# Two-layer hybrid mixer kernel: the gate matmuls of the recurrent part from fp32 to three fp32r passes, and their place in the order

## The chip, the cores and the metric

The kernel runs on one core of a Trainium2 chip, as one program. The metric is the device time of one execution in microseconds. The engines are TensorE (PE in the profile; PEld are its weight loads), VectorE (DVE), ScalarE (ACT), GpSimd (POOL) and SyncE (SP), which issues most of the DMAs.

## The reference

A backbone of two layers over 1024 latent tokens and 256 context tokens, width 1024. Each layer normalizes and modulates its input, projects it to 2048 columns, mixes tokens in three parallel ways, projects back, and runs a gated feed-forward part with a convolution. Context tokens run through the first layer fully; in the second only their keys, values and recurrent states are needed. The change is in the recurrent mixer, 512 channels wide:

```python
u = dwconv(r, conv_w, conv_b, 2, 1)                  # r: first 512 projected columns
for d, reverse in enumerate((False, True)):          # two directions
    r_ = sigmoid(blockdiag(u, w_a[d]) + b_a[d])      # 8 blocks of 64 x 64
    i_ = sigmoid(blockdiag(u, w_x[d]) + b_x[d])
    log_a = -8 * r_ * softplus(-lam[d]);  a = exp(log_a)
    h[d] = scan(a, sqrt(1 - exp(2 * log_a)) * i_ * u)   # h_t = a_t h_(t-1) + drive_t
y = (h[0] + h[1]) * gelu(gate)                       # gate: next 512 projected columns
```

The two other mixers are attention: one global, one over a window, with two key/value heads and four query heads each.

## The kernel before

Tokens lie along the free axis: 256 of context (chunk c), then two chunks of 512 latent tokens (A and B), 1280 in all (TOK). Most matmuls compute fp32 products in three passes: each operand is split into a high part, rounded to fp32r by a ScalarE copy, and a low part, the rest, by a subtraction on VectorE or GpSimd (`split`, L319); `gemm` (L326) adds high x high, high x low and low x high into one PSUM bank.

`in_proj` (L853) holds the stage in question. It goes over four channel tiles `ct` of 128 channels. Each has two projections of 24 matmuls per chunk: the raw half (i even) and the gate half (i odd). `lru_evac` copies the raw half from PSUM into `lru_raw`, and the gate half through a Gelu into `lru_gate`. `lru_conv` makes `u` from the raw half (one ScalarE activation and three VectorE operations for each of two token ranges). `lru` runs both directions: for each, two gate products of `u` with the block-diagonal weights `bd` in three chunks (L817, fp32 matmuls, banks 4 and 5 in turn), each evacuated by a tanh, then activations and VectorE operations, ending in the scan. `lru_out` adds the directions (L841) and multiplies by the gate (L842). In layer 1 both leave the context columns out.

Then four groups of head columns are projected, token by token tile (ten tiles of 128 tokens; groups 0 and 2 leave out the two context tiles in layer 1): group 0 gives the queries `gq`, group 1 keys and values `gk` and `gv`, groups 2 and 3 go to DRAM by way of `st`. Each tile is 24 matmuls of 256 columns and one or two evacuations. Attention follows; its first score products (out of `K` and `Q`) are the end of the stage.

Banks 0 to 3 take the projections: in the order 3, 0, 1, 2 for the channel tiles (L886), 0, 1, 2, 3 for the head groups. In the first tile chunk A of projections 0, 1 and 2 is done first, in banks 0, 1 and 2; the third of these (the raw half of the second tile) is evacuated late, by the `late` entry.

On-chip memory is laid out by hand. In the region X0, slots of 5120 bytes hold: slot 0 the raw half, slot 1 `u`, slot 2 the gate, slots 3 to 6 in turn the three work tiles A, B and C of a direction. There is one raw, one `u` and one gate slot, so each waits for its last reader of the tile before. Behind slot 6, at X0 + 35872, lies `mraw`, the buffer for modulation weights (`mod_fill`, 24 steps of PE work that are put among the others as fillers; their results are used in the output projection). In the region H0, eight slots of 5120 bytes hold the residual `h`. It is saved to DRAM (`save`) so that its slots can be reused: `bd` in slots 6 and 7, the recurrent result `ya` in 0 to 3, `gq` in 4 and 5, `gk` in 6, `gv` in 7. Group 1's weights for the second half of the rows lie at X0 and X0 + 35872 (`ex`, L868).

The order on each engine is not that of the text. A scheduler takes the instructions with the text's order as priority, and its own estimate of when each is ready, and writes one fixed sequence per engine and DMA queue; it inserts the waits that overlapping memory needs. On the chip each engine goes through its sequence in order.

Of the kernel before, what the change touches and what calls it, by code (L numbers as in the profile page):

```python
# [9 lines left out]
F32 = mybir.dt.float32  # L10
F32R = mybir.dt.float32r
# [5 lines left out]
P = 128  # L17
# [4 lines left out]
TOK = SEQ + CTX  # L22
# [269 lines left out]
class Builder:  # L292
# [378 lines left out]

    def mod_fill(self):
        for s in (*range(16, 32), *range(40, 48)):
            self.mod_step(0, s, self.sb("mraw", [P, 1024], F32, self.X0 + 35872) if s < 32 else None)
            yield

    def rstd_from(self, out, v, t):
# [72 lines left out]

    def load_bd(self, l):
        nc = self.nc
        bd = self.sb("bd", [P, 2, 2, 4, P], F32, self.H0 + 6 * 5120)
        nc.gpsimd.memset(bd, 0.0)
        for a, name in ((0, "lru_w_a"), (1, "lru_w_x")):
            for o in range(2):
                for d in range(2):
                    src = self.io[name][l, d].rearrange("(t o) c e -> o c t e", o=2)[o]
                    nc.sync.dma_start(bd[64 * o:64 * o + 64, a, d, :, 64 * o:64 * o + 64], src)
        self.bd = bd  # L760

    def proj(self, l, i, ch, x, w, ring):
        n = CHUNKS[ch][1]
# [38 lines left out]
                self.stt(u[:, c0:c0 + n], r[:, p0 + s:p0 + s + n], cw(i), u[:, c0:c0 + n], OP.mult, OP.add)  # L802
        return u

    def lru(self, l, ct, u):
        nc = self.nc
        lc = self.lcol[:, l]
        hs = []
        for d in range(2):
            j = 4 * d + ct  # L810
            A, B, C = (self.lslot(3 + (self.lru_i + q) % 4) for q in range(3))
            self.lru_i += 3
            for dst, a in ((A, 0), (B, 1)):
                for ch in ("c", "A", "B"):
                    c0, n = CHUNKS[ch]
                    ps = self.bank((4, 5))
                    self.mm(ps[:, :n], self.bd[:, a, d, ct], u[:, c0:c0 + n], True, True)  # L817
                    self.act(dst[:, c0:c0 + n], ps[:, :n], AF.Tanh, scale=0.5, bias=lc[:, a, j:j + 1])
            self.act(C, A, AF.Tanh, scale=lc[:, 2, j:j + 1], bias=lc[:, 2, j:j + 1])
            self.act(A, A, AF.Exp, scale=lc[:, 3, j:j + 1], bias=lc[:, 3, j:j + 1])  # L820
            self.stt(C, A, 1.0, C, OP.add, OP.mult)
            nc.vector.tensor_scalar(A, C, -1.0, 1.0, op0=OP.mult, op1=OP.add)
            self.stt(C, A, 1.0, C, OP.add, OP.mult)
            self.act(C, C, AF.Sqrt, scale=0.25)
            self.stt(B, B, 1.0, u, OP.add, OP.mult)
            nc.vector.tensor_tensor(B, B, C, op=OP.mult)
            scan = nc.vector.tensor_tensor_scan
            if d == 0:
                scan(C, A, B, 0.0, OP.mult, OP.add)
            else:  # L830
                scan(C[:, :CTX][:, ::-1], A[:, :CTX][:, ::-1], B[:, :CTX][:, ::-1], 0.0, OP.mult, OP.add)
                scan(C[:, CTX:][:, ::-1], A[:, CTX:][:, ::-1], B[:, CTX:][:, ::-1], C[:, 0:1], OP.mult, OP.add)
            hs.append(C)
        self.hs = hs
# [18 lines left out]
    def in_proj(self, l, x, wc, fillers):  # L853
# [4 lines left out]
        def save(ks):  # L858
            c0 = 0 if need else CTX
            for k in ks:  # L860
                nc.sync.dma_start(self.hsp[k][:, c0:], self.h[k][:, c0:])

        save((6, 7))
        self.load_bd(l)
        wp = {}

        def load(grp):
            ex = {1: (self.X0, self.X0 + 35872), 3: (self.X0 + 10240, self.X0 + 14336)}  # L868
            wp[grp] = [self.weight(win[:, 4 * q:4 * q + 4, 1024 + 256 * grp:1280 + 256 * grp], 4, 256,
                                   ex[grp] if q and grp in ex else (None, None), pool_lo=grp != 1)  # L870
                       for q in range(2)]

        done = set()
        for ct in range(4):
            for i in (2 * ct, 2 * ct + 1):
                if i not in wc:
                    wc[i] = self.lru_weight(l, i)
                if i == 7:
                    load(0)
                for ch in ("A", "B", "c"):  # L880
                    if ch == "c" and i % 2 and not need:
                        continue
                    for i2 in ((0, 1, 2) if (i, ch) == (0, "A") else (i,)):
                        if (i2, ch) not in done:
                            done.add((i2, ch))
                            ps = self.proj(l, i2, ch, x, wc[i2], (i2,) if (i, ch) == (0, "A") else (3, 0, 1, 2))  # L886
                            if (ct, i2) == (0, 2):
                                late = ps
                            else:
                                self.lru_evac(l, *ps)  # L890
                    if ch != "B":
                        next(fillers, None)
                if i % 2 == 0:
                    u = self.lru_conv(l, ct)
                    if ct == 0:
                        self.lru_evac(l, *late)
                    self.lru(l, ct, u)
                    save(((0,), (1, 4), (2, 5), (3,))[ct])
            self.lru_out(l, ct)
            if l == 0 and ct == 1:  # L900
                for _ in self.params_load(1, self.MS0):
                    pass
                self.lru_cols(1)
# [3 lines left out]
        for grp in range(4):  # L907
# [4 lines left out]
            for tt in range(10):  # L912
# [3 lines left out]
                o = (tt if tt < 2 else (tt - 2) % 4) * P  # L916
                ps = self.bank((0, 1, 2, 3))[:, :256]
                i = 0
# [612 lines left out]
```

## Time and profile before

| what | value |
|---|---|
| median of 3 runs | 3006.15 us (3005.23 to 3008.45) |
| the profiled execution: its time | 3004.2 us |
| its span, first to last instruction | 3002.4 us |
| mean granted TensorE clock | 0.981 of full speed |
| busy: PE, DVE, ACT, POOL | 94%, 72%, 50%, 45% |
| recurrent part with head groups, layer 0 | about 92 to 363 us |
| the same, layer 1 | about 1698 to 1948 us |

The busy share is an average over stages with different limits. Idle time that a view shows stands ahead of an instruction, with the engine whose signal ended it. A line number may be that of a helper: L308 is every activation, L311 every matmul, L317 every scalar_tensor_tensor of VectorE, so instructions are told apart by the names of what they write and read: `bank<-lru,bd` is a gate matmul, `bank<-w,a` a head group's matmul on latent tokens, `bank<-w,ac` on context tokens, `bank<-a,w` and `bank<-ac,w` a channel tile's projection, `lru` any tile of the recurrent part. A fp32 matmul shows as two instructions. Where a row merges several instructions (x2), its shape is that of the first.

### The profile page before, as it was taken

How to read it: one execution, taken by the hardware profiler on the slowest of the kernel's cores; microseconds unless marked ns; L12 is line 12 of the kernel's file. 1: busy time of each engine (PE TensorE's matmuls, PEld its weight loads, DVE VectorE, ACT ScalarE, POOL GpSimd, SP SyncE). 2: the span in 40 equal slices, each digit the busy share in tenths (PEclk: the TensorE clock that was granted, in tenths of full speed). 3: DMA queues.
4: the chain of work that ended last, by engine and by line, in shares of the span. 5: the costliest groups of instructions: out<-in, count | busy, mean ns of one | idle time of the engine just before them, and what ended most of it. 6: DMA issues, size and time to landing. Idle time of an engine off the chain costs nothing. (4 is left out here: it accounts for less than half of the span.)

```text
span 3002.4 us, 38806 instructions
## 1 busy us (share of the span) xinstructions
PE 2823.1 (94%) x14523; PEld 2265.2 (75%) x14523; DVE 2156.1 (72%) x2890; ACT 1497.1 (50%) x2426; POOL 1354.4 (45%) x814
## 2 busy tenths in 40 slices
PE   7999988899899999999999989988998999999998
PEld 4668955668788888887778768956676788887887
DVE  5666798775876666676756766898727877776666
ACT  4675477843433333365542666378834433344114
POOL 1211166642455555547773210067652666666110
PEclk8999999999999999999999999999999999999999
DMA  7422200132333333375452211200031344335321
GB/s 267 142 65 92 78 1 18 37 105 75 106 111 111 111 111 111 111 246 169 160 185 85 73 33 36 74 22 11 22 123 60 114 125 124 119 122 196 106 77 57
DMA packets 295774, 299.56 MB, mean 100 GB/s; under 512 B 16586, under 2 KB 250658, under 8 KB 295586
## 3 DMA queue, kind: packets, MB, share of 16 engines
q1 hardware_dynamic: 271538, 246.59, 26.0%
q10 hardware_dynamic: 24048, 50.50, 4.8%
q8 instruction: 114, 1.87, 0.3%
q14 instruction: 74, 0.61, 0.1%
HBM read 243.02 MB, written 54.02 MB: 99 GB/s over the span
## 5 line engine op out<-in xcount | busy, mean ns | idle before, releaser
L322 POOL TENSOR_TENSOR w<-wr,w 128x1024 fp32r<-128x1024 f32 (+1 forms) x220 | 565.5, 2593 | 220.1 <-ACT w L308 198.2
L311 PE MATMUL bank<-y,w 128*128 128x512 f32 (+1 forms) x2688 | 576.0, 374 | 14.6 <-DVE h L317 12.7
L311 PEld LDWEIGHTS bank<-y,w 128*128 128x128 f32 x2688 | 468.4, 191 | 111.6 <-DVE h L317 15.4
L311 PE MATMUL bank<-xt,w 128*128 128x512 f32 x2112 | 513.2, 396 | 23.2 <-ACT p L308 8.0
L311 PEld LDWEIGHTS bank<-xt,w 128*128 128x128 f32 x2112 | 398.8, 191 | 115.4 <-POOL w L322 9.7
L1131 POOL TENSOR_TENSOR ph<-pf,ph 128x512 fp32r<-128x512 f32 x256 | 340.3, 1351 | 299.2 <-PE bank L311 178.0
L317 DVE SCALAR_TENSOR_TENSOR h<-bank,mod,h 128x512 f32<-128x512 f32 (+1 forms) x448 | 300.1, 685 | 188.8 <-PE bank L311 188.0
L317 DVE SCALAR_TENSOR_TENSOR cv<-fr,fcol,cv 128x1282 f32<-128x1282 f32 (+1 forms) x176 | 375.4, 2190 | 70.0 <-ACT cv L308 70.0
L308 ACT ACTIVATE w<-wr 128x1024 fp32r<-128x1024 f32 (+1 forms) x220 | 222.8, 1016 | 393.1 <-POOL wr L178 234.6
L311 PE MATMUL bank<-a,w 128*128 128x512 f32 x1536 | 387.8, 404 | 11.0 <-ACT a L308 3.5
L311 PE MATMUL bank<-x,w 128*128 128x512 f32 x1584 | 379.8, 390 | 1.8 <-DVE x L317 1.1
L311 PEld LDWEIGHTS bank<-a,w 128*128 128x128 f32 x1536 | 286.9, 190 | 86.9 <-issue 12.4
L311 PEld LDWEIGHTS bank<-x,w 128*128 128x128 f32 x1584 | 296.3, 188 | 63.3 <-issue 1.5
L322 POOL TENSOR_TENSOR w<-raw,w 128x1024 fp32r<-128x1024 f32 x38 | 101.6, 2676 | 382.2 <-ACT w L308 370.8
L311 PE MATMUL bank<-ph,V 128*128 128x512 f32 (+1 forms) x768 | 243.2, 415 | 5.5 <-POOL ph L1131 2.5
L311 PEld LDWEIGHTS bank<-ac,w 128*128 128x128 f32 x1536 | 195.8, 192 | 15.7 <-issue 4.8
L311 PE MATMUL bank<-ac,w 128*128 128x256 f32 x1536 | 204.0, 286 | 3.0 <-ACT lru L308 1.7
L311 PE MATMUL bank<-w,a 128*128 128x256 f32 x1536 | 201.3, 287 | 2.6 <-ACT gq L308 2.6
L178 POOL TENSOR_TENSOR wr<-wr,wr 128x512 f32<-128x512 f32 x44 | 57.8, 1313 | 321.4 <-DVE wr L178 204.2
L311 PEld LDWEIGHTS bank<-w,a 128*128 128x128 f32 x1536 | 191.4, 192 | 10.9 <-issue 6.2
L1073 DVE TENSOR_REDUCE mt<-bank 128x1 f32<-128x512 f32 (+2 forms) x336 | 168.5, 534 | 37.1 <-PE bank L311 34.2
L658 POOL TENSOR_TENSOR macc<-macc,mt 128x512 f32<-128x512 f32 x112 | 158.9, 1419 | 59.7 <-ACT mt L308 31.1
(212 smaller groups left out, 3964.2 us busy)
## 6 DMA issues: line engine op xcount, KB each, us to landing
wr<-in_w_up SPq DMA_DIRECT2D x154, 512.0 KB
wr<-in_w_down SPq DMA_DIRECT2D x44, 512.0 KB
mraw<-in_w_mod SPq DMA_DIRECT2D x32, 512.0 KB
raw<-in_w_in SPq DMA_DIRECT2D x32, 512.0 KB
mraw<-in_w_mod ACTq DMA_DIRECT2D x64, 256.0 KB
y_spill<-cv ACTq DMA_DIRECT2D x22, 641.0 KB
yr<-y_spill SPq DMA_DIRECT2D x22, 641.0 KB
y_spill<-cv ACTq DMA_DIRECT2D x22, 512.0 KB
```

The lines of the kernel that those rows point to most:

```text
L178: tt = lambda e, out, x, y, op: e.tensor_tensor(out, x, y, op=op)
L308: return self.nc.scalar.activation(out, in_, func, **kw)
L311: return self.nc.tensor.matmul(out, lhsT, rhs, start=start, stop=stop)
L317: return (eng or self.nc.vector).scalar_tensor_tensor(out, in0, scalar, in1, op0=op0, op1=op1)
L322: self.nc.gpsimd.tensor_tensor(lo, src, hi.bitcast(F32), op=OP.subtract)
L658: nc.gpsimd.tensor_tensor(acc, acc, t, op=OP.add)
L1073: nc.vector.reduce_max(mt[:, 4 * u + s:4 * u + s + 1], ps[:, :n], axis=AX.X)
L1131: nc.gpsimd.tensor_tensor(pl, pf, ph.bitcast(F32), op=OP.subtract)
```

## The change

The weights `bd` are split once per layer into a high and a low part, in H0 slots 4 to 7: the raw weights and then their low part at H0 + 20480, the high part 8192 bytes further. `u` is split for each channel tile, the high part `uh` into X0, where the raw half lay, the low part `ul` to X0 + 35872, where `mraw` lay. Each gate product is three fp32r matmuls. `mraw` goes to the end of H0's slot 7 (H0 + 36864). The residual's slots 4 to 7 are saved first. In the two middle channel tiles the gate half is projected, in the text's order, ahead of the gate products; in the first and last the products come first as before. The late evacuation of the first tile comes behind that tile's gate products. `gq`, `gk`, `gv` and group 1's weights stay where they are.

```diff
--- before.py
+++ after.py
@@ -671,7 +671,7 @@
 
     def mod_fill(self):
         for s in (*range(16, 32), *range(40, 48)):
-            self.mod_step(0, s, self.sb("mraw", [P, 1024], F32, self.X0 + 35872) if s < 32 else None)
+            self.mod_step(0, s, self.sb("mraw", [P, 1024], F32, self.H0 + 4 * 5120 + 16384) if s < 32 else None)
             yield
 
     def rstd_from(self, out, v, t):
@@ -750,14 +750,16 @@
 
     def load_bd(self, l):
         nc = self.nc
-        bd = self.sb("bd", [P, 2, 2, 4, P], F32, self.H0 + 6 * 5120)
+        o = self.H0 + 4 * 5120
+        bd = self.sb("bd", [P, 2, 2, 4, P], F32, o)
+        hi, lo = (self.sb("bd", [P, 2, 2, 4, P], F32R, o + 8192 * q) for q in (1, 0))
         nc.gpsimd.memset(bd, 0.0)
         for a, name in ((0, "lru_w_a"), (1, "lru_w_x")):
             for o in range(2):
                 for d in range(2):
                     src = self.io[name][l, d].rearrange("(t o) c e -> o c t e", o=2)[o]
                     nc.sync.dma_start(bd[64 * o:64 * o + 64, a, d, :, 64 * o:64 * o + 64], src)
-        self.bd = bd
+        self.bd, self.bd_raw = (hi, lo), bd
 
     def proj(self, l, i, ch, x, w, ring):
         n = CHUNKS[ch][1]
@@ -802,7 +804,7 @@
                 self.stt(u[:, c0:c0 + n], r[:, p0 + s:p0 + s + n], cw(i), u[:, c0:c0 + n], OP.mult, OP.add)
         return u
 
-    def lru(self, l, ct, u):
+    def lru(self, l, ct, u, uh, ul):
         nc = self.nc
         lc = self.lcol[:, l]
         hs = []
@@ -814,7 +816,7 @@
                 for ch in ("c", "A", "B"):
                     c0, n = CHUNKS[ch]
                     ps = self.bank((4, 5))
-                    self.mm(ps[:, :n], self.bd[:, a, d, ct], u[:, c0:c0 + n], True, True)
+                    self.gemm(ps[:, :n], [([z[:, a, d, ct] for z in self.bd], [z[:, c0:c0 + n] for z in (uh, ul)])])
                     self.act(dst[:, c0:c0 + n], ps[:, :n], AF.Tanh, scale=0.5, bias=lc[:, a, j:j + 1])
             self.act(C, A, AF.Tanh, scale=lc[:, 2, j:j + 1], bias=lc[:, 2, j:j + 1])
             self.act(A, A, AF.Exp, scale=lc[:, 3, j:j + 1], bias=lc[:, 3, j:j + 1])
@@ -860,7 +862,7 @@
             for k in ks:
                 nc.sync.dma_start(self.hsp[k][:, c0:], self.h[k][:, c0:])
 
-        save((6, 7))
+        save((4, 5, 6, 7))
         self.load_bd(l)
         wp = {}
 
@@ -892,10 +894,16 @@
                         next(fillers, None)
                 if i % 2 == 0:
                     u = self.lru_conv(l, ct)
+                    uh = self.sb("uh", [P, TOK], F32R, self.X0)
+                    ul = self.sb("ul", [P, TOK], F32R, self.X0 + 35872)
+                    self.split(uh, ul, u)
+                    if ct == 0:
+                        self.split(*(z.rearrange("p a d t n -> p (a d t n)") for z in (*self.bd, self.bd_raw)))
+                if i == 2 * ct + (0 < ct < 3):
+                    self.lru(l, ct, u, uh, ul)
                     if ct == 0:
                         self.lru_evac(l, *late)
-                    self.lru(l, ct, u)
-                    save(((0,), (1, 4), (2, 5), (3,))[ct])
+                    save(((0,), (1,), (2,), (3,))[ct])
             self.lru_out(l, ct)
             if l == 0 and ct == 1:
                 for _ in self.params_load(1, self.MS0):
```

## Rows read from the trace of the kernel before

**Rows 1.** Busy line of the page: engine, us (share of the span), x instructions.

```profile
PE 2823.1 (94%) x14523; PEld 2265.2 (75%) x14523; DVE 2156.1 (72%) x2890; ACT 1497.1 (50%) x2426; POOL 1354.4 (45%) x814
```

**Rows 2.** Table of stretches: from:to, us, busy us (x instructions) by engine, PEclk, DMA share, GB/s.

```profile
257.00:345.00 88.00, 88.00 (x728) 84.96 (x729) 63.00 (x113) 33.49 (x81) 11.13 (x4) 1.00 0.24 79
...
1796.00:1840.00 44.00, 39.63 (x224) 32.06 (x223) 30.86 (x24) 29.86 (x38) 2.38 (x1) 0.96 0.09 26
...
1840.00:1862.00 22.00, 22.00 (x140) 17.95 (x139) 10.46 (x7) 17.68 (x25) 2.19 (x1) 1.00 0.06 21
```

**Rows 3.** Timeline, ScalarE, layer 1: start, us, engine, line, operation, xcount [idle before <-releaser].

```profile
1712.59 1.05 ACT L308 ACTIVATE lru<-bank,lcol 128x256 f32<-128x256 f32 x2
...
1725.47 1.28 ACT L308 ACTIVATE lru<-lru 128x1280 f32<-128x1280 f32 x1 [2.29 <-DVE lru L317]
...
1754.65 1.06 ACT L308 ACTIVATE lru<-bank,lcol 128x256 f32<-128x256 f32 x2
...
1795.97 1.05 ACT L308 ACTIVATE lru<-bank,lcol 128x256 f32<-128x256 f32 x2 [1.78 <-DVE ya L841]
...
1798.34 1.09 ACT L308 ACTIVATE lru<-bank 128x512 f32<-128x512 f32 x2
...
1839.61 1.06 ACT L308 ACTIVATE lru<-bank,lcol 128x256 f32<-128x256 f32 x2 [2.83 <-DVE ya L841]
...
1866.41 1.12 ACT L308 ACTIVATE gq<-bank 128x128 f32<-128x128 f32 x6
...
1897.65 0.38 ACT L308 ACTIVATE st<-bank 128x256 f32<-128x256 f32 x1 [2.50 <-PE bank L311]
```

**Rows 4.** The same timeline view, VectorE, layer 1.

```profile
1707.23 2.84 DVE L317 SCALAR_TENSOR_TENSOR lru<-lru,pcol,lru 128x256 f32<-128x256 f32 x3 [0.70 <-ACT lru L308]
...
1789.01 1.48 DVE L826 TENSOR_TENSOR lru<-lru,lru 128x1280 f32<-128x1280 f32 x1
...
1790.42 1.28 DVE L317 SCALAR_TENSOR_TENSOR lru<-lru,pcol,lru 128x1024 f32<-128x1024 f32 x1
...
1792.33 2.35 DVE L832 TENSOR_TENSOR_SCAN lru<-lru,lru,lru 128x1024 f32<-128x1024 f32 x1
...
1794.71 1.23 DVE L841 TENSOR_TENSOR ya<-lru,lru 128x1024 f32<-128x1024 f32 x1
```

**Rows 5.** The same timeline view, TensorE, layers 0 and 1.

```profile
256.94 1.13 PE L311 MATMUL bank<-lru,bd 128*128 128x512 f32 x2
...
1698.31 0.87 PE L311 MATMUL bank<-a,w 128*128 128x512 f32 x3
...
1767.29 1.02 PE L311 MATMUL bank<-lru,bd 128*128 128x512 f32 x2
...
1786.83 0.59 PE L311 MATMUL bank<-lru,bd 128*128 128x256 f32 x2
...
1861.52 1.12 PE L311 MATMUL bank<-lru,bd 128*128 128x512 f32 x2
...
1947.73 1.57 PE L311 MATMUL bank<-Q,K 128*128 128x512 f32 x6
```

**Rows 6.** Groups by form, TensorE: 215.5 to 256.9, then 1812 to 1861.5.

```profile
L311 PE MATMUL bank<-w,a 128*128 128x256 f32 x111 | 15.8, 295 | 0.9 <-ACT gq L308 0.9
...
L311 PE MATMUL bank<-w,ac 128*128 128x256 f32 x48 | 8.3, 312 | 1.0 <-ACT lru L308 1.0
...
L311 PE MATMUL bank<-w,a 128*128 128x256 f32 x216 | 31.9, 302 | 0.0
...
L311 PE MATMUL bank<-w,ac 128*128 128x256 f32 x37 | 5.2, 285 | 1.4 <-DVE w L324 1.4
```

**Rows 7.** Instructions on tile bd: duration min/median/max in ns, first and last start.

```profile
L754 POOL MEMSET bd<- x2: 1806/1808/1810, 96.8 to 1702.0; 128x2048 f32 x2
```

**Rows 8.** The same view, tile h_spill, 60 to 135.

```profile
L861 SPq DMA_DIRECT2D h_spill<-h x8: 319/320/424, 63.7 to 87.7; - x8
```

**Rows 9.** Waits of TensorE, 1698 to 1866: us in total, times, longest.

```profile
PE bank L311 <- DVE lru L317: 6.3, 2, 4.2
```

## The prediction

> **What bounds the kernel now.** First the busy line of the page: TensorE is busy 94% of the span, VectorE 72%, ScalarE 50% [rows 1]. That is an average, so the second view is the table of stretches around the edited stage [rows 2]. In layer 1's third tile (1796 to 1840) PE is busy 39.63 of 44 us, in its fourth (1840 to 1862) 22.00 of 22, and after layer 0's last gate 88.00 of 88. So PE has little idle time to give back here. The third view, the timelines, shows what sets the pace underneath. The tanh that opens a channel tile starts at 1712.59, 1754.65, 1795.97 and 1839.61 [rows 3]: 42, 41 and 44 us per tile, whatever PE does. It is a chain of ScalarE and VectorE steps, through two directions per tile. The third tile's first tanh ends a wait of ScalarE for the add at L841 [rows 3, 4], the fourth's likewise. PE fills the gaps of this chain with projections, towards the end with the first head group's (group 0, output gq). When the chain lets go of PE at its last gate (256.94 in layer 0, 1861.52 in layer 1 [rows 5]), PE works off the remaining head-group tiles without a gap, and attention's first score products start behind them at 1947.73 [rows 5]. So the stage's length is (time of the last gate) + (head-group tiles still undone then) x (time of one). One tile of 24 matmuls takes 0.38 + 2.50 = 2.88 us, the rhythm of its evacuations [rows 3].
>
> How many are undone: up to the last gate layer 0 has done 111 + 48 = 159 of their matmuls, 159 / 24 = 6.6 tiles of 40; layer 1 216 + 37 = 253, 10.5 tiles of 36 [rows 6].
>
> **The change, part by part.**
> *Three passes.* 64 gate matmuls of 512 columns and 32 of 256 over both layers. An fp32 one of 512 is two instructions, 1.02 us together, of 256 0.59 us; three fp32r of 512 take 0.87 us [rows 5]. Saved: 64 x 0.15 + 32 x 0.07 (half of it) = 12 us of PE time, between 0 and 64 x 0.255 + 32 x 0.13 = 20 (a quarter of each pair). By "FP8 and Floating Point Precision" of the Trainium skill, section TensorE Precision Notes, true fp32 is four passes, so that three would save the quarter, 20 us; the rows give less, and no run here shows three-pass gates. It is worth its time only where PE sets the end, which by the formula above is after the last gate, where there are no gates. I take 0 for it; if PE did set the pace, it is the faster rival's gain.
>
> *The split of u*, eight times: one ScalarE copy of 1280 columns (1.28, nearest row a 1280-column activation without pointer operands) and one VectorE subtraction (1.48) [rows 3, 4], between the convolution and the gates.
>
> *The split of bd*, twice: 2048 columns, 2048 / 1280 times those: 2.0 and 2.4 us.
>
> First tile: the convolution ends at 1707.23 + 2.84 = 1710.07 [rows 4], the first tanh starts at 1712.59. Now 1.28 (u) + 2.0 (bd high) + 2.4 (bd low) follow before the third pass: 1715.8, and the tanh at 1715.9: +3.3 us. Bounds: 0 (both hide behind the table load and evacuations there) and 5.7 (their full sum). Layer 0 has the same steps; I take the same.
>
> Each later tile: before, the convolution ends at 1790.42 + 1.28 = 1791.70, then VectorE scans to 1792.33 + 2.35 = 1794.68 and adds to 1794.71 + 1.23 = 1795.94, and the tanh starts [rows 4]. VectorE is full there, so its 1.48 us falls into the chain: +1.5 us a tile, the value I take. Low end 0: the gate half is already projected for the two middle tiles, its Gelu (1.09 for two [rows 3]) leaves the tanh sequence with the table load ahead of it, and pays for it. High end 4.3: the subtraction also comes behind the output's product, as long as that add (1.2), and the evacuation of the next raw half, which now waits, pushes the next convolution by about 1.6. Sum per layer 3.3 + 3 x 1.5 = 8 us, bounds 3 and 16.
>
> *The high part uh lies in the raw buffer.* The next tile's raw half can't be evacuated before the last gate of this tile has read uh, some 22 us into the tile (1861.52 against 1839.61 [rows 3, 5]), where it followed the convolution at once. Queued behind: that half's three memsets on POOL, its evacuations on ACT, and the three banks they hold of four. I follow each bank's queue: PE starves in the second half of each tile, but every projection is still done before the fourth tile's chain needs it; so 0 to the end, and one group of 24 matmuls of 512, 24 x 0.29 = 7 us (0.87 / 3 each, an upper value), per layer if one slips.
>
> *bd moves from h slots 6 and 7 to 4 to 7.* This is the term that decides. gq is slots 4 and 5. In the kernel before, gq's tiles are evacuated while the gates still run; now they alias bd's low and high parts and wait for the last gate. Is it the whole tile that waits, or only the columns in use? The add at L841 of layer 1 reads columns 256 on (1024 of them [rows 4]), yet the tanh that writes columns 0 to 255 of that slot waits for it [rows 3]; and three k/v tiles of group 1, over bd, are evacuated together at 1866.41 only, after the last gate [rows 3], although the blocks under the first of them belong to earlier tiles. Both say: the whole tile. So PE can do one gq tile per free bank, 4 in all, and then stops until the last gate. Layer 0: (6.6 - 4) x 2.88 = 7.5 us more behind the gate; layer 1: (10.5 - 4) x 2.88 = 18.7.
>
> *Also*: the weights of group 1's second half go to the slots of uh and ul, so they wait for the last gate too; up to 8 gq tiles cover that. mraw moves onto h7 and waits for its save and for the norm's reads: the saves are all issued by 87.7 and the norm's last reads end where bd's memset starts, 96.8 [rows 7, 8], so the modulation steps start some 10 us later; they are short PE work that the new gaps take in, and they are due only before the output projection. Saving h4 and h5 first moves two DMAs on SP ahead of bd's memset, no more: all eight are issued before it anyway. No DMA is added. The order of gate half and gates in the two middle tiles: 0, the timeline shows both interleaved already. The late evacuation behind the first tile's gates: in the bank queues above.
>
> Sum, on the profiled execution: 3004.2 + (8 + 7.5) + (8 + 18.7) = 3046.4. The median of the runs is 3006.15, 1.95 more: 3048.
>
> **The rivals.**
> *Faster: PE sets the pace all the way.* If gq's tiles are evacuated column by column, the chain is no longer than now, and the last gates come no later after the stage's start than at present, then PE's 12 us count, and with gate projections ahead of the gates go the two waits for the convolution, 6.3 us in layer 1 [rows 9]: 3006 - 18 = 2988. For it: PE's 94%, its full stretches. Against it: the tanh waits for whole tiles. The point from which it decides is the time of the last gate. "Perfetto Trace Analysis" of the Trainium skill, Identifying the Most-Contended Engine, says to optimize the engine of highest occupancy first, which is PE; by that rule this case would hold. Chance 0.20.
>
> *Slower by less: aliasing goes by columns, the chain as forecast.* Then some 7.8 tiles of layer 0 and 8 of layer 1 (all of its group 0; group 1 waits for weights) are done at the last gate: 8 - 1.2 x 2.88 and 8 + 2.5 x 2.88, with 2.3 us for the weights' split: 4.5 + 17.5 = 22, 3028. Against it the same rows. 0.15.
>
> *Slower by more: each tile's start takes the high end.* 16 us of chain per layer in place of 8: 3064. For it: VectorE has no gap before the add at L841. 0.11.
>
> *Nothing measurable*: shorter gates and the lost tiles cancel, 3006. 0.06.
>
> **How the numbers follow.** The forecast has 0.48 and by its bounds (chain 3 to 16 a layer) reaches from 3038 to 3064. Two tenths may stay outside: most of the faster case below 3000 (0.15) and some of the slowest above 3066 (0.05). Range 3000 to 3066. Faster by over 0.2% (6 us, about what a measurement here tells from no change) 0.20, within it 0.06, slower 0.74.
>
> **What would show it.** Right: gq evacuations only after the last gate, none beside the gates; 4 gq tiles' matmuls before it, in both layers; PE idle stretches of several us before each tile's first gate and before the last; the opening tanhs 42 to 46 us apart and the fourth's some 8 us later; first scores later by 15 and by 27 more. Wrong: gq copies between the gates of the fourth tile (columns), or tiles less than 41 us apart, or a last gate no later than now.

## The result, and the profile after

The changed kernel takes 3074.69 us (median; 3071.62 to 3076.53) against 3005.74 of the kernel before on the same chip: ratio 1.0229, interval [1.0217, 1.0242], some 69 us slower. The forecast was 3048, its range ended at 3066: the sign was right, the size 27 us short. The profiled execution has a span of 3074.7 us against 3002.4; it is the slowest of the four, and the one of the kernel before is faster than its median, so the traces lie 72 us apart. One execution, of the version below that has everything at once with the order undone, took 11120 us and is left out of its median.

The busy line of the page, kernel after, answers to [rows 1]:

```profile
PE 2840.0 (92%) x14619; PEld 2297.3 (75%) x14619; DVE 2160.3 (70%) x2900; ACT 1507.9 (49%) x2433; POOL 1353.1 (44%) x814
```

As an average it shows next to nothing: TensorE is busy a little longer, in a longer span. The stretches of the edited stage say more. Columns as in [rows 2]; the first fence is the kernel before, to the last gate of layers 0 and 1:

```profile
84.00:256.90 172.90, 161.70 (x892) 114.88 (x890) 117.34 (x138) 120.58 (x155) 25.15 (x20) 1.00 0.33 98
1655.00:1861.50 206.50, 188.85 (x926) 146.99 (x925) 146.13 (x160) 138.87 (x186) 35.44 (x31) 0.98 0.13 42
```

The kernel after, each layer to its last gate, a short stretch behind it, and the rest up to the first score product:

```profile
84.00:273.80 189.80, 156.15 (x858) 119.71 (x857) 124.94 (x143) 123.01 (x153) 27.62 (x21) 0.92 0.27 85
273.80:290.00 16.20, 11.85 (x79) 9.95 (x79) 12.22 (x10) 9.04 (x13) 0.00 (x0) 0.68 0.29 97
290.00:398.20 108.20, 107.16 (x891) 103.90 (x888) 56.73 (x123) 35.15 (x92) 9.56 (x4) 1.00 0.21 68
1690.00:1912.00 222.00, 176.50 (x827) 142.75 (x826) 152.04 (x166) 140.66 (x182) 36.18 (x30) 0.90 0.12 39
1912.00:1930.00 18.00, 13.92 (x89) 13.42 (x90) 11.42 (x9) 9.54 (x14) 0.00 (x0) 0.72 0.10 30
1930.00:2021.70 91.70, 90.50 (x734) 89.13 (x733) 61.58 (x122) 31.52 (x81) 10.62 (x4) 1.00 0.19 60
```

Up to the last gate of layer 0, TensorE stands for 33.7 us (189.80 - 156.15) where it stood for 11.2; behind it, it has a gap and a granted clock of 0.68, then full work at 1.00. The head group's matmuls done by then, in layer 0 (84 to 273.8) and layer 1 (1754 to 1912), grouped by form as in [rows 6]:

```profile
L311 PE MATMUL bank<-w,ac 128*128 128x256 f32 x48 | 7.7, 303 | 0.2 <-ACT lru L308 0.2
L311 PE MATMUL bank<-w,a 128*128 128x256 f32 x48 | 6.2, 285 | 1.2 <-ACT lru L308 1.2
...
L311 PE MATMUL bank<-w,a 128*128 128x256 f32 x96 | 14.5, 305 | 1.4 <-ACT lru L308 1.4
```

96 matmuls are four tiles, in both layers, as forecast. What happens at the last gate, TensorE's timeline (answers to [rows 5]):

```profile
273.81 0.50 PE L311 MATMUL bank<-uh,bd 128*128 128x512 f32 x1 [2.98 <-ACT lru L308]
...
278.86 6.03 PE L311 MATMUL bank<-w,a 128*128 128x256 f32 x27 [3.90 <-ACT gq L308]
...
398.19 0.63 PE L311 MATMUL bank<-Q,K 128*128 128x512 f32 x2
...
1912.01 0.50 PE L311 MATMUL bank<-uh,bd 128*128 128x512 f32 x1 [4.07 <-ACT lru L308]
...
1917.07 14.39 PE L311 MATMUL bank<-w,a 128*128 128x256 f32 x96 [4.07 <-ACT gq L308]
...
2021.64 0.63 PE L311 MATMUL bank<-Q,K 128*128 128x512 f32 x2
```

and ScalarE's there, layer 1:

```profile
1913.77 0.68 ACT L308 ACTIVATE lru<-bank,lcol 128x512 f32<-128x512 f32 x1
1914.34 1.45 ACT L308 ACTIVATE lru<-lru,lcol 128x1280 f32<-128x1280 f32 x1
1915.69 1.05 ACT L308 ACTIVATE w<-raw 128x1024 fp32r<-128x1024 f32 x1
1916.63 1.20 ACT L308 ACTIVATE gq<-bank 128x256 f32<-128x256 f32 x4
```

All four banks' gq tiles are copied at once, after the last gate, behind an exp and a weight copy that stand ahead of them; TensorE waits 4 us for them. The first scores come 35.1 us later in layer 0 (398.19 against 363.07 in the kernel before, the first row below) and 73.9 later in layer 1 (2021.64 against 1947.73 [rows 5]). POOL's first addition in layer 1's norm, which leads into its stage, is the second row in the kernel before and the third in the kernel after:

```profile
363.07 1.11 PE L311 MATMUL bank<-Q,K 128*128 128x512 f32 x4
...
1645.58 1.29 POOL L698 TENSOR_TENSOR acc<-acc,sq 128x512 f32<-128x512 f32 x1 [22.11 <-ACT sq L308]
...
1682.20 1.29 POOL L698 TENSOR_TENSOR acc<-acc,sq 128x512 f32<-128x512 f32 x1 [22.06 <-ACT sq L308]
```

From layer 0's first score it is 1282.5 us to that addition before and 1284.0 after. So of the 73.9 us all but 1.5 lie in the two stages of the edit. Each layer has two terms, the time of the last gate and what lies behind it. For all kernels below they are read the same way (last set of gates, first score product; "between" is the stretch from layer 0's first score to layer 1's norm, and layer 1's last gate is counted from there). Each row is one execution; those of one kernel lie 2 to 12 us apart. In us more than before:

| kernel | layer 0: last gate | behind it | between | layer 1: last gate | behind it | sum |
|---|---|---|---|---|---|---|
| forecast | 8 | 7.5 | 0 | 8 | 18.7 | 42 |
| after | 16.9 | 18.2 | 1.5 | 13.9 | 23.4 | 74 |
| before, alias alone | 4.5 | 10.2 | 0.7 | 1.5 | 22.3 | 39 |
| before, order alone | 9.4 | 0 | 2.2 | 0.1 | 0 | 12 |
| after, both aliases eased | 17.2 | 3.4 | -0.1 | 16.0 | 13.3 | 50 |
| the same, one pass | 16.6 | 3.0 | 6.6 | 11.6 | 14.2 | 52 |
| the same, one pass, no low parts | 12.7 | 5.8 | 0.6 | 6.1 | 13.6 | 39 |
| after, tanh's table early | 14.3 | 17.2 | 3.2 | 10.6 | 23.4 | 69 |

### The profile page after: what moved, and what is told of

It is laid out like the page before. It is cut to its first block, busy times and chain, and to the rows that moved or that the text cites. A ratio compares the mean times of both kernels' runs of the same rounds, so it can differ in the third digit from the quotient of the medians.

```text
span 3074.7 us, 39036 instructions
## 1 busy us (share of the span) xinstructions
PE 2840.0 (92%) x14619; PEld 2297.3 (75%) x14619; DVE 2160.3 (70%) x2900; ACT 1507.9 (49%) x2433; POOL 1353.1 (44%) x814
## 5 line engine op out<-in xcount | busy, mean ns | idle before, releaser
L311 PE MATMUL bank<-y,w 128*128 128x512 f32 (+1 forms) x2688 | 575.3, 373 | 10.8 <-DVE h L317 10.6
L311 PE MATMUL bank<-a,w 128*128 128x512 f32 x1536 | 381.8, 402 | 18.7 <-ACT lru L308 10.0
L311 PE MATMUL bank<-w,a 128*128 128x256 f32 x1536 | 202.1, 290 | 10.5 <-ACT gq L308 8.0
```

Of the source, the lines that this page charges most:

```text
L311: return self.nc.tensor.matmul(out, lhsT, rhs, start=start, stop=stop)
```

## The experiments

Every time stands beside the kernel before on the same chip; "+47" is the ratio's excess times 3006. Each edit makes the planner write a new order for all engines, so that a run shows one edit and some us of reordering. The code fences show the deciding lines of an edit, not all of it.

**Where gq and uh lie.** Four kernels. The alias alone, on the kernel before (fp32 gates, no split; the saves in the changed order, too):

```
-        bd = self.sb("bd", [P, 2, 2, 4, P], F32, self.H0 + 6 * 5120)
+        bd = self.sb("bd", [P, 2, 2, 4, P], F32, self.H0 + 4 * 5120)
```

> The kernel before, its fp32 gates kept, no split anywhere, with only bd moved from h slots 6 and 7 to 4 and 5 (under gq) and the saves in the changed kernel's order. By the formula of the prediction (four gq tiles until the last gate) +7.5 in layer 0 and +18.7 in layer 1: 3032. With the stop that the changed kernel shows behind its last gates (gq copied 4 us late, TensorE at half clock for its first run) 18 and 23: 3047. If the alias costs nothing by itself: 3003 to 3010.

3044.15, ratio 1.0122 [1.0103, 1.0142]: +37. The last gates and the gq copies of its layer 1, first TensorE, then ScalarE:

```profile
1878.33 2.08 PE L311 MATMUL bank<-lru,bd 128*128 128x512 f32 x2 [6.50 <-ACT lru L308]
1882.59 1.65 PE L311 MATMUL bank<-w,a 128*128 128x256 f32 x6 [2.18 <-ACT gq L308]
```

```profile
1881.59 0.67 ACT L308 ACTIVATE lru<-bank,lcol 128x512 f32<-128x512 f32 x1
1882.16 1.20 ACT L308 ACTIVATE gq<-bank 128x256 f32<-128x256 f32 x4
```

The same picture without any three-pass gate: TensorE stands 6.5 us ahead of the last set of gates and 2.2 behind it, four gq tiles are held back, and there are 10.2 and 22.3 us more behind the gates, 2.7 and 3.6 above the formula.

The other way, on the changed kernel: gq's first half and the fourth product change places (with their later users, and h slot 3 saved at the start), so that five gq tiles lie off bd; then uh of the first three tiles out of the raw buffer, into h slot 3; then both:

```
-        y = self.sb("ya", [P, TOK], F32, self.H0 + ct * 5120)
+        y = self.sb("ya", [P, TOK], F32, self.H0 + (ct + ct // 3) * 5120)
-        self.gq = [hs(4, [P, 5, 256]), hs(5, [P, 5, 256])]
+        self.gq = [hs(3, [P, 5, 256]), hs(5, [P, 5, 256])]
```

```
-                    uh = self.sb("uh", [P, TOK], F32R, self.X0)
+                    uh = self.sb("uh", [P, TOK], F32R, self.H0 + 3 * 5120 if ct < 3 else self.X0)
```

> The changed kernel with the other alias eased: gq's first half (slot 4) and the fourth product (slot 3) change places, so that gq's first five tiles no longer lie over bd; uh stays in the raw buffer. Theory A: in layer 0 gq's tiles go on ahead of the last gate and the stop behind it goes (18 us measured there), in layer 1 three tiles more are done (7 instead of 4, 8.6 us) and part of the stop stays: 20 to 30 us less, 3045 to 3055. Theory B: PE starves ahead of the last gate for other reasons (banks held by raw halves that wait) and reaches gq no sooner: 3065 to 3075.

> The changed kernel with one alias undone: the high part uh of the first three channel tiles lies in h slot 3 (free until the fourth tile's product) and no longer in the raw buffer. The changed kernel is 3075. Theory A (the splits sit in the chain of ScalarE and VectorE; gq waits for bd): the next raw half can be evacuated at once, PE idles less, but the opening tanhs and the last gates stay where they are, and gq's four-tile limit too: 3069 to 3077. Theory B (the raw buffer is the missed term: conv of the next tile comes late because its raw half waits for the last gate): each of six tile starts comes about 4 us earlier, last gates about 12 us earlier in each layer: 3045 to 3055.

> Both aliases undone at once, the rest of the change as it is. If the two aliases are all of the loss but for the splits in the chain: 3010 to 3035 by theory A (what stays is 15 us of chain in each layer at most), under 3010 if the raw buffer made the chain late (theory B). If neither alias matters and the splits are all: 3060 to 3075.

gq eased: 3053.79, 1.0156 [1.0136, 1.0176], +47, so 22 us come back. uh moved: 3076.24, 1.0231 [1.0216, 1.0246], nothing. Both: 3053.90, 1.0154 [1.0137, 1.0171], as gq alone, and 19 us above the 3035 that I expected at most: 33 us of chain and 17 behind the gates are left (table). In the last, gq is copied between the gates again, at 238.27 where the last gate comes at 274:

```profile
238.27 0.38 ACT L308 ACTIVATE gq<-bank 128x256 f32<-128x256 f32 x1 [1.23 <-PE bank L311]
```

The raw buffer costs nothing; gq's place is worth 22 us even half undone (layer 1 has 7 tiles done by the last gate, not 10.5, and keeps 13.3 us). What neither touches is the lateness of the last gates.

**The order**, alone on the kernel before, and undone in the version with both aliases eased:

```
                 if i % 2 == 0:
                     u = self.lru_conv(l, ct)
+                if i == 2 * ct + (0 < ct < 3):
                     if ct == 0:
                         self.lru_evac(l, *late)
                     self.lru(l, ct, u)
```

> The kernel before with only the order of the change: in the two middle tiles the gate half's projection stands ahead of the gates. fp32 gates, no split, all buffers as before (3007). Theory A (the order is worth nothing, the planner interleaves both anyway): 3001 to 3013. Theory C (the order is a cost: the chain's gates queue behind 20 projection matmuls in each middle tile, about 4 us a tile): 3015 to 3025. Theory D (it is the gain that the change hoped for, hidden by the aliases): 2990 to 3000.

> The version with both aliases undone (3054) and the order of the change undone, so that what is left of the change is the splits, the three passes and the moved mraw. Theory A: 3048 to 3060, the splits are what is left. Theory C (order costs): 3030 to 3045. Theory D: over 3062.

Alone 3017.29, 1.0034 [1.0022, 1.0046]: +10, 9.4 of the 12 in its trace at layer 0's last gate. Undone 3057.95, 1.0168 [1.0149, 1.0187], no better than 1.0154 [1.0137, 1.0171]. So it costs a little alone and nothing that can be told apart inside the change. That the planner interleaves each version anew may be why; no run shows it.

**Passes and low parts**, on the version with both aliases eased. One pass, high by high, the low parts computed and not read (two passes left out); then the low parts not computed either:

```
-                    self.gemm(ps[:, :n], [([z[:, a, d, ct] for z in self.bd], [z[:, c0:c0 + n] for z in (uh, ul)])])
+                    self.mm(ps[:, :n], self.bd[0][:, a, d, ct], uh[:, c0:c0 + n], True, True)
```

> The version with both aliases undone (3054), gates in one pass (high by high; the two passes with a low part are left out), while both low parts are still computed. It takes 192 of 288 gate matmuls away, some 40 us of TensorE time. Theory A (TensorE does not set the pace up to the last gate, only the wait of the first gates for the low parts goes, as they need not be read): 3035 to 3050, of it some 4 us at the first tile of each layer. Theory P (TensorE's work ahead of the last gate sets the pace): 3015 to 3030.

> As the one-pass version, and the low parts are no longer computed (ten VectorE subtractions less, eight of 1.48 and two of 2.29 us). Theory A (VectorE's subtraction stands in the chain ahead of the add that opens the next tile): 8 x 1.5 = 12 us less than the one-pass version. Rival (VectorE has slack there): within 4 us of the one-pass version.

One pass 3049.07, 1.0139 [1.0120, 1.0159]; no low parts 3041.68, 1.0115 [1.0095, 1.0135]. Taking 192 of 288 gate matmuls away gives 5 us, within the intervals: TensorE does not set the pace up to the last gate. By "Perfetto Trace Analysis" of the Trainium skill, Identifying the Most-Contended Engine, the engine of highest occupancy is the one to work on first, and for TensorE the busy share of its weight loads (PEld) is to be taken, not that of its matmuls. Taken so up to the last gates of the version that this run starts from, the rule still names TensorE, but barely: PEld is busy 126.54 us in layer 0 and 152.25 in layer 1, ScalarE 124.07 and 145.32, VectorE 120.24 and 151.93. The run speaks against working on TensorE in this stage.

Leaving the low parts out too gives 7 us more, at the edge of the intervals, and the last gates come 3.9 us earlier in layer 0 and 5.5 in layer 1 (table). That is less than the 12 us that I expected with the subtractions all in the chain, and more than the rival's 4.

The low part of u on POOL, in the version of everything below with two mraw buffers:

```
-                    self.split(uh, ul, u)
+                    self.split(uh, ul, u, pool_lo=True)
```

> As the last, with u's low part computed on POOL instead of VectorE (eight subtractions of 1.48 us leave VectorE). If VectorE's 1.48 us a tile are in the chain and POOL's step hides: 8 us less in the six later tiles than the last version. If POOL's longer subtraction then is what the first gates wait for (POOL's split of 1024 columns took 2.4 us, so some 3 us for 1280, 1.5 more than VectorE's): within 4 us of the last version, or up to 10 more where VectorE's scans beside it stretch (4.9 instead of 2.8 us beside POOL in layer 0).

3056.16, 1.0174 [1.0145, 1.0204], 10 us slower than its base (3046.53 on the same chip; each of its four executions is slower than each of the base's). POOL and VectorE at the end of its third tile, layer 1:

```profile
1878.07 3.02 POOL L322 TENSOR_TENSOR ul<-lru,uh 128x1280 fp32r<-128x1280 f32 x1 [13.99 <-ACT uh L308]
```

```profile
1878.24 5.00 DVE L834 TENSOR_TENSOR_SCAN lru<-lru,lru,lru 128x1024 f32<-128x1024 f32 x1
```

The scan takes 5.00 us beside POOL's subtraction (2.35 alone [rows 4]): in this tile more is given back than the 1.47 us saved.

**The first tile and the modulation steps**, each alone on the changed kernel: bd's halves exchanged and its split ahead of the convolution; mraw back in its place for twelve of its sixteen steps (not fourteen, as the expectation has it), with ul of the first three tiles in h slot 3; mraw in two places by turns (h7's end and h slot 3):

```
-        bd = self.sb("bd", [P, 2, 2, 4, P], F32, o)
-        hi, lo = (self.sb("bd", [P, 2, 2, 4, P], F32R, o + 8192 * q) for q in (1, 0))
+        bd = self.sb("bd", [P, 2, 2, 4, P], F32, o + 8192)
+        hi, lo = (self.sb("bd", [P, 2, 2, 4, P], F32R, o + 8192 * q) for q in (0, 1))
```

```
-            self.mod_step(0, s, self.sb("mraw", [P, 1024], F32, self.H0 + 4 * 5120 + 16384) if s < 32 else None)
+            self.mod_step(0, s, self.sb("mraw", [P, 1024], F32, self.X0 + 35872 if s < 28 else self.H0 + 4 * 5120 + 16384) if s < 32 else None)
-                    ul = self.sb("ul", [P, TOK], F32R, self.X0 + 35872)
+                    ul = self.sb("ul", [P, TOK], F32R, self.H0 + 3 * 5120 if ct < 3 else self.X0 + 35872)
```

```
+            self.mod_step(0, s, self.sb("mraw", [P, 1024], F32, self.H0 + (4 * 5120 + 16384 if s % 2 else 3 * 5120)) if s < 32 else None)
```

> The changed kernel (3075) with bd's split ahead of the convolution and its halves exchanged (the loaded array at the upper 8192 bytes), so that its memset waits for h7 again and comes behind POOL's last step of the norm. If the first tile's lateness (5.4 us in layer 0, 8 in layer 1) is the row of u split, bd high and bd low behind the convolution (4.2 us of bd in each layer), and the memset ahead of the norm's step (2.5 us in layer 1): first gates 3 to 4 us earlier in layer 0 and 5 to 7 in layer 1, 3062 to 3068. If bd's DMA, started 1.7 us later in layer 1, is what the first gates wait for: 3072 to 3078.

> The changed kernel (3075) with mraw back in its place at the end of the X0 region (14 of 16 steps) and ul of the first three tiles in h slot 3 instead. Theory M (mraw's move starts the modulation steps 10 us late, and TensorE, which takes its instructions in order, stands 13 us behind their DMAs among layer 0's gates and has 24 of their matmuls left behind the last gate): layer 0's first two tiles 5 to 6 us shorter, 2 us less behind the gate: 3064 to 3070, all of it in layer 0. Theory 0 (as in the prediction, the steps fall into idle time): 3072 to 3078.

> The changed kernel (3075) with two buffers for the modulation steps (h7's free end and h slot 3, by turns). Theory M (gates stand in TensorE's order behind a step that waits for its DMA, and the scan stands behind ms in VectorE's): TensorE's waits for mraw fall from 12.9 us to under 4, layer 0's last gate comes 5 to 8 us earlier, 3066 to 3070, nothing changes in layer 1. Rival (the waits fill time in which the chain of ScalarE and VectorE was busy anyway): 3072 to 3078.

bd early: 3071.93, 1.0226 [1.0209, 1.0243]; mraw back: 3078.82, 1.0252 [1.0232, 1.0273]; two mraw buffers: 3075.98, 1.0234 [1.0210, 1.0259]. None differs from the changed kernel by more than the intervals. What bd's memset does on POOL in layer 1 is plain, first the kernel after, then the one with bd's halves exchanged:

```profile
1736.91 1.82 POOL L756 MEMSET bd<- 128x2048 f32 x1 [0.21 <-DVE nt L317]
1738.68 3.51 POOL L737 TENSOR_TENSOR ac<-nt,ac 128x256 fp32r<-128x256 f32 x1
```

```profile
1738.73 0.75 POOL L737 TENSOR_TENSOR ac<-nt,ac 128x256 fp32r<-128x256 f32 x1 [1.23 <-ACT ac L308]
1739.41 1.82 POOL L756 MEMSET bd<- 128x2048 f32 x1
```

In the changed kernel bd lies over h4 and h5 and so may be cleared before the norm's last step, which it delays; exchanged, u's high part is copied 3.9 us sooner (counted from the norm's first step), but ScalarE still takes bd's split behind u's, and the first gates gain 2.3. Layer 0 gives that back (last gate 17.5, in the terms of the table, against 16.9), layer 1's last gate comes 3.5 us sooner (10.4 against 13.9).

TensorE's waits for mraw in layer 0 fell from 12.9 to 5.8 us with two buffers, and the last gate did not move (274.1 against 273.8). One of these waits does reach the chain in the kernel after, in layer 0's first tile; TensorE, then ScalarE:

```profile
134.83 1.08 PE L520 MATMUL bank<-mraw,cond 128*32 128x256 f32 x8 [3.40 <-DMA mraw<-in_w_mod]
135.84 0.80 PE L311 MATMUL bank<-uh,bd 128*128 128x512 f32 x1
```

```profile
137.53 0.69 ACT L308 ACTIVATE lru<-bank,lcol 128x512 f32<-128x512 f32 x1 [2.76 <-PE bank L311]
```

The gate stands behind a step that waits for its DMA, and its tanh waits 2.76 us for the gate. With two buffers the stretch from the first scan to the add of this tile is 3.4 us shorter, but the first opening comes 1.2 us later, this tile's first half (opening to the end of the first scan) is 0.8 longer, and the third tile, opening to add, 2.2. So my theory, that these waits set the last gate, falls; what mraw's move costs by itself stays open.

**The tanh's table.** A tanh of eight columns, its result unused, makes ScalarE load the table ahead:

```
                     self.split(uh, ul, u)
+                    if ct:
+                        self.act(self.sb("pre", [P, 8], F32, self.X0 + 41024), uh[:, :8].bitcast(F32), AF.Tanh)
```

> The changed kernel (3075) with one tanh of eight columns of uh, its result unused, behind the split of each of the six later tiles, so that ScalarE loads the tanh's table ahead of its wait for the add. The number of table loads stays. Theory T (the load behind the wait is in the chain of each later tile): each opening tanh 0.1 us behind the add's end instead of 1.37, last gates 3 to 4 us earlier per layer, 3066 to 3069. Rival (the opening waits for the gates' passes or the next step gives it back): 3072 to 3077.

3068.59, 1.0210 [1.0193, 1.0227]: 6 us less than the changed kernel, as the theory had it, though the intervals touch; in its trace the last gates come 2.6 and 3.3 us earlier (table). Four of the six later tiles open 0.09 to 0.39 us behind the add; the other two stay at 2.07 and 4.49. ScalarE at the opening of layer 1's fourth tile, after, then with the early tanh; the add at L843 ends at 1888.11 and 1885.21:

```profile
1888.19 1.28 ACT L308 ACT_TABLE_LOAD   x1 [5.18 <-DVE ya L843]
1889.48 1.05 ACT L308 ACTIVATE lru<-bank,lcol 128x256 f32<-128x256 f32 x2
1890.55 1.28 ACT L308 ACT_TABLE_LOAD   x1
```

```profile
1880.12 1.28 ACT L308 ACT_TABLE_LOAD   x1
1881.41 0.21 ACT L308 ACTIVATE pre<-uh 128x8 f32<-128x8 f32 x1
1885.30 1.06 ACT L308 ACTIVATE lru<-bank,lcol 128x256 f32<-128x256 f32 x2 [3.68 <-DVE ya L843]
```

**Everything at once**: gq eased (in layer 1 numbered from its first tile in use, so that five of its eight tiles lie off bd and three fit the banks), mraw back, bd early; that with the order undone; with two mraw buffers; and with the early tanh.

```
+        self.g0 = 0 if need else 2
-                    self.act(self.gq[tt // 5][:, tt % 5], ps)
+                    self.act(self.gq[(tt - self.g0) // 5][:, (tt - self.g0) % 5], ps)
```

> All at once: gq's first half and the fourth product exchanged, gq in layer 1 numbered from its first tile in use (so that its eight tiles fit five places and the banks), mraw back, bd split early; three passes and the order as in the changed kernel. If the terms add up: 3054 (gq eased) - 8 (mraw) - 9 (bd) - 3 to 5 (layer 1's last gq tiles) = 3030 to 3036, what stays being the low parts (12 us by the runs with one pass) and the order. If they hide behind each other: 3040 to 3054.

> The same with the order of the change undone. Theory C (the order costs 9 us in layer 0's two middle tiles, as it did on the kernel before): 3020 to 3027. If the order is worth nothing here (as in the version with both aliases undone, where undoing it gave 3058 against 3054): within 5 us of the version with the order. Under 3006 only if the three passes pay once everything about them is out of the way; I don't expect that.

> The version with all of it (3044) and two mraw buffers. Theory M: 3036 to 3040. Rival: 3042 to 3047.

> The version with all of it (3044) and the same early tanh. Theory T: 3035 to 3039. Rival: 3041 to 3047. Under 3006 by neither.

3044.11, 1.0138 [1.0121, 1.0155]; 3043.07, 1.0132 [1.0116, 1.0149]; 3046.53, 1.0138 [1.0112, 1.0165]; 3042.94, 1.0124 [1.0106, 1.0142]. In all four the rival of the theory came out. The terms don't add up: 41 us stay of 69, undoing the order and the second buffer change nothing, and the early tanh, worth 6 us on the changed kernel, is within the intervals here. No version with three passes comes near 3006.

## Why the prediction was right in sign and short in size

Two steps failed by size: what lies behind the last gate (26.2 us forecast in both layers, 41.6 measured) and the chain up to it (16 forecast, 30.8 measured).

*The stage's formula* held: the loss is the last gates' lateness plus undone head-group tiles, layer by layer: 72.4 us by these terms and 1.5 between the stages, against 72.3 in the span.

*gq over bd* was the step that decides, and its mechanism is shown: no gq copy before the last gate, four tiles done, 37 us from the alias alone, 22 back when eased. The size failed. "So PE can do one gq tile per free bank, 4 in all, and then stops until the last gate" stops too early: TensorE stands on behind the gate, until ScalarE, after the exps and the weight copy, reaches the copies (3.90 and 4.07 us), and its first run behind the two gaps goes partly at 1.2 GHz (PEclk 0.68 and 0.72 in the short stretches, 1.00 behind them), about 3 us in each layer (the first 27 matmuls of layer 0 took 6.03 us; at 2.88 / 24 = 0.12 each it would be 3.2). In layer 0 24 more matmuls of the modulation steps are left, 2 us. Together with the forecast that is 16.4 for 18.2 in layer 0 and 25.8 for 23.4 in layer 1: right in sum, 2 us off in each layer.

*The chain*: 8 us a layer taken, 16.9 and 13.9 measured. (The upper bound of 16 holds the first tile at its middle value; with that tile's own 5.7 it is 18.6.) The failed step is "Each later tile", "+1.5 us a tile, the value I take": it puts nothing between the add and the tanh, and its low end has a Gelu that "leaves the tanh sequence with the table load ahead of it, and pays for it". The table load came into the chain instead: in the kernel before the third tile's tanh starts 0.03 us after the add [rows 3, 4], as in five of six later tiles, in the changed one 1.37 after it in four of six later tiles. In the other two the subtraction stands behind the add, and the tanh starts 2.07 and 4.55 us after it: in the first it waits for the gates, which wait for the low part, in the second ScalarE takes the gate half's copies first, and these wait for the product behind the subtraction:

```profile
1797.38 0.60 ACT L308 ACTIVATE lru<-bank 128x512 f32<-128x512 f32 x1 [7.44 <-DVE ya L844]
...
1799.30 1.05 ACT L308 ACTIVATE lru<-bank,lcol 128x256 f32<-128x256 f32 x2
```

Summed over three tiles and against before, the openings' distance from the add grew by 4.7 us in layer 0 and 5.9 in layer 1; the run with the early tanh takes 4.9 of these 10.6 away, so that much is the load. The low part's 1.5 a tile is right where the subtraction stands right ahead of the add (1885.51 in the fence below), as in three of six tiles; tile by tile it can't be read from the times, and without all low parts 7 us go over both layers, not 12. The first tile was short: openings at 112.77 and 1756.62, 5.9 late in layer 0 and, counted from its norm, 7.4 in layer 1, not 3.3, since the steps follow each other almost in full and, in layer 1, the norm's last step comes 3.9 us late behind bd's memset. VectorE at the same opening as above, kernel after:

```profile
1883.24 2.35 DVE L834 TENSOR_TENSOR_SCAN lru<-lru,lru,lru 128x1024 f32<-128x1024 f32 x1
1885.51 1.47 DVE L324 TENSOR_TENSOR ul<-lru,uh 128x1280 fp32r<-128x1280 f32 x1
1886.89 1.22 DVE L843 TENSOR_TENSOR ya<-lru,lru 128x1024 f32<-128x1024 f32 x1
```

What is left of the lateness lies in the stretches from an opening to its tile's add at L843 and from the last opening to the last gate: 6.3 us in layer 0 (5.9 + 4.7 + 6.3 = 16.9) and 0.6 in layer 1 (7.4 + 5.9 + 0.6 = 13.9). These sums hide larger parts of both signs, the subtractions among them. One that the prediction has no term for is VectorE beside POOL. Four steps of the convolution in layer 1's second tile, then in its third, and POOL beside the first four:

```profile
1827.69 7.56 DVE L317 SCALAR_TENSOR_TENSOR lru<-lru,pcol,lru 128x256 f32<-128x256 f32 x4
...
1876.55 3.27 DVE L317 SCALAR_TENSOR_TENSOR lru<-lru,pcol,lru 128x256 f32<-128x256 f32 x4
```

```profile
1826.49 3.55 POOL L322 TENSOR_TENSOR w<-raw,w 128x1024 fp32r<-128x1024 f32 x1 [6.24 <-ACT w L308]
1831.36 2.41 POOL L322 TENSOR_TENSOR w<-raw,w 128x1024 fp32r<-128x1024 f32 x1 [1.33 <-ACT w L308]
```

With 4.3 us of this and 1.5 of subtraction the second half of that tile (first scan to add) is 5.7 us longer than before; the first halves of tiles one and two are 6.2 us shorter, and why is not shown.

*What was costed at nothing*: the raw buffer (0, right), the three passes (5 us at most, within the intervals, with two of them left out), mraw's move (no gain from undoing it, though one wait for it stands in the chain), the order (0 inside the change; 10 alone, so wrong as a part by itself). The bound of what the passes save has a slip that changes nothing: a quarter of 0.59 is 0.15, not 0.13, and the bound 21 us.

*The rivals*: faster fell with the last gates; column-wise aliasing fell with the four tiles; "each tile's start takes the high end" had the chain's size (16 a layer) and would have come to 3064; but only layer 1's second tile went its way, the rest came from the table load and the first tile, so that its size is in part luck; and it missed the longer stop behind the gates. The rule cited for the faster rival goes by TensorE's weight loads: over the span of the kernel before they are busy 75% against VectorE's 72% [rows 1], so it did name TensorE; up to the last gates alone it hardly does, with 114.88 us against VectorE's 117.34 and ScalarE's 120.58 in layer 0, and 146.99 against 146.13 and 138.87 in layer 1.

Not settled: layer 0's last gate stays 15 to 21 us late in the four versions with everything at once. What of it is the planner's order was not separated: reordering may move that gate by several us (278.8 with mraw back, 273.8 in the changed kernel).

## What to carry to other kernels

Before a buffer is moved, list every tile that will lie over it, and price the wait to the end of the copy that frees it, with what stands ahead of that copy in its engine's order and the slower clock of the first run behind the gap, not just the work that is held back. Where a chain of ScalarE and VectorE sets the pace, price an edit by what it puts between the last step and the next opening (a subtraction, a table load behind a wait, a copy that waits for another step), look at what POOL does beside VectorE, and give TensorE's saved passes nothing, however busy it looks.

## What was not expected of the hardware

In these rows a table load is held by the wait that stands ahead of its function: it takes 1.28 us, and the tanh starts 1.37 behind the event, or 0.03 in the kernel before, where the table was loaded ahead. "ScalarE: Activation LUTs" of the Trainium skill, What ACT_TABLE_LOAD costs, gives 1283 ns for the load, with which the rows agree, and a further 1380 for a drain, which these rows don't show: the tanh at 1889.48 starts 0.01 us after its load's end (1888.19 + 1.28), and the next load at 1890.55 0.02 us after the tanh's (1889.48 + 1.05).

VectorE and POOL stop each other. In the kernel after, tile one of layer 0, VectorE and then POOL:

```profile
154.55 2.35 DVE L834 TENSOR_TENSOR_SCAN lru<-lru,lru,lru 128x1024 f32<-128x1024 f32 x1
...
156.94 3.50 DVE L843 TENSOR_TENSOR ya<-lru,lru 128x1280 f32<-128x1280 f32 x1
...
160.47 1.49 DVE L844 TENSOR_TENSOR ya<-ya,lru 128x1280 f32<-128x1280 f32 x1
```

```profile
155.49 3.60 POOL L322 TENSOR_TENSOR w<-raw,w 128x1024 fp32r<-128x1024 f32 x1 [5.21 <-ACT w L308]
```

POOL's split, 2.41 us at 1831.36 above, takes 3.60 from 155.49: 1.4 of it lie beside the scan. It ends at 159.09; the add beside it takes 3.50, 2.0 more than the product behind it, and 1.35 of it, about its own 1.49, lie behind POOL's end. "SBUF — State Buffer" of the Trainium skill, Who interferes with whom, says that a VectorE operation with two SBUF inputs and a GpSimd one that reads SBUF hold a shared port for the whole instruction while the other stands; these rows agree.
